# A hybrid attention layer on one core: other signs in its seven-product matrix form, one weight sum made by an adding transfer, and three reorderings in attention

## The chip, the core and the metric

The kernel runs on one core of a Trainium2 chip. The core has a matrix engine (PE, with its weight loads shown apart as PEld), a vector engine (DVE), a scalar engine (ACT), a general engine (POOL) and SyncE (SP), each with its own instruction queue; they meet at semaphores. Weights come from device memory by DMA into SBUF, matmuls write PSUM, and DVE and ACT read both. The metric is the device time of one execution in microseconds (us): 362.66 us before the change, the median of three runs from 362.60 to 362.94.

## The reference

One decoder layer in float32: RMSNorm, one wide projection, two attention mixers (NSA: compressed, selected and sliding-window keys; MoBA: block sparse), gates, an output projection, and a feed-forward block with squared ReLU between two more norms. There are 256 tokens and a model width of 1024.

```python
h = rmsnorm(x, norm1_g[layer])
proj = h @ w_in[layer]
...
gm = jax.nn.sigmoid(g_m.astype(jnp.float32)).astype(x.dtype)
g_nsa = gm[..., :D_MODEL]
g_moba = gm[..., D_MODEL:]
mixed = g_nsa * (y_nsa @ w_up_nsa[layer]) + g_moba * (y_moba @ w_up_moba[layer])
x = x + mixed @ w_out[layer]
h2 = rmsnorm(x, norm2_g[layer])
u = jax.nn.relu(h2 @ w_ff1[layer])
x = x + (u * u) @ w_ff2[layer]
...
return rmsnorm(x, norm_f_g)
```

With 256 tokens all selected and windowed keys lie within the causal mask, so the kernel computes two causal softmaxes per NSA head and one per MoBA head.

## The kernel before, in words

**Exact float32 from three products.** Each weight chunk (`raw`, 1 MB, three buffers, loaded by SP) is split in two: ACT copies a rounded part into `whi` (line 114), DVE subtracts it and leaves the rest in `wlo` (line 116). The activations are split the same way, and PE does three matmuls per block: hi by hi, hi by lo, lo by hi.

**Slots.** The program is a list of slots, one per weight chunk (`CHUNKS`): `kva`, `kvb`, `q`, `qm`, `km`, `vm`, eight `gm`, `upn`, `upm`, four `wout`, then the feed-forward chunks. `run_slot` issues a slot's matmuls one after another; everything else (splits, copies, loads, attention) is put among them by `at(pos, f, ...)`: it is issued when the share `pos` of the slot's matmuls has been issued, and ties keep the order of writing. No scheduler changes this: every engine runs its instructions in that order, and an instruction that waits holds up what stands behind it on its engine.

**Early part.** After the `kva` chunks, `evac_tm` copies each half of the accumulator twice over into `kcd` (line 326) and the rest into `kva` (line 329). `cmp_gather` (line 419) turns `kcd` on PE, `gather_evac` adds position terms on DVE.

**Attention.** Six units `d` of two heads' pairs each run through slots 9 to 21 (`unit_events`, line 648): in an odd slot scores on PE (`d_scores`), maxima on DVE, exponentials on ACT (line 581), and the product with the values of the unit before (`d_pv`, `d_yevac`); in the even slot after it the normalising on DVE (`d_norm`, line 595) and the transposes on PE (`d_trans`, line 611), whose results ACT (line 613) and DVE (line 615) copy back. Slot 9 holds the second `km` chunk, slot 12 the first `gm` chunk. At half of slot 9, `evac_tm` copies the first half of MoBA's keys from PSUM (line 329, `qtm`) and frees an accumulator that the `vm` chunk needs.

**Feed-forward.** An ff1 slot (48 matmuls of 256 columns) makes 256 hidden columns; ACT squares them (`squares`, tile `aq`). The product with `w_ff2` is done for the first 14 chunks by a form of two-by-two block multiplication with seven products in place of eight (`SEVEN`, line 1011): sums of blocks of `aq` and sums of weight blocks (`sums`, line 974) are multiplied, the seven products pile up in seven PSUM banks over all 14 chunks, and `combine` (line 1028) adds them into the output once at the end. So each pair of slots (a seven-product slot and an ff1 slot) has on DVE: the weight sums into tile `wt` (lines 984, 988, 990), the activation sums (line 982), the rest `sl` of the single blocks (line 999), the rest of the ff1 chunk (line 116), the rest of `wt` (line 1008) and the rest `al` of the activations (line 958). ACT makes the rounded parts (lines 997, 114, 1006, 956). `wt` has two buffers, as have `sh`, `sl`, `ah`, `al`; `whi` and `wlo` have three. The last two ff2 chunks are multiplied in the plain way, and the output is normalised (`final_a`, `final_b`; the power is done on POOL, line 1171) and stored.

```python
    SEVEN = (("1", 0, 0), ("7", 4, 4), ("5", 3, 3), ("6", 5, 5), ("2", 2, 1), ("3", 6, 2),
             ("4", 1, 6))
```

Each entry is a product's name, the index of the block of `A` (blocks 1 to 7 of `aq`, split) and of the weight block (0 to 2 the single blocks, 3 to 6 those of `wt`).

Of the kernel before, what the change touches and what calls it, by code (L numbers as in the profile page):

```python
# [8 lines left out]
F32 = mybir.dt.float32  # L9
F32R = mybir.dt.float32r  # L10
AF = mybir.ActivationFunctionType
ALU = mybir.AluOpType
# [9 lines left out]
NSEVEN = 14  # L22
# [23 lines left out]
def hybrid_layer(ctx: ExitStack, tc: tile.TileContext, gxd, w, w1c, small, const, gf, out):  # L46
# [178 lines left out]
    def at(pos, f, *a):  # L225
        ev.append((pos, f, a))
# [94 lines left out]
    vm = ap_.tile([128, 2, 512], F32, name="vm")  # L321
    tm = {"kva": kva, "kvb": kvb, "vm": vm}

    def evac_tm(sec, t, acc, n):
        if sec == "kva":
            act.activation(kcd[:, t], acc[:, 0:256].rearrange("p (a d) -> p a d", a=4)[:, :, None, :]
                           .to_broadcast([128, 4, 2, 64]), AF.Copy, scale=rstd[:, t:t + 1])
            acc, n = acc[:, 256:384], 128
        act.activation(tm[sec][:, t, :], acc[:, :n], AF.Copy, scale=rstd[:, t:t + 1])  # L329

# [317 lines left out]
    def unit_events(s):  # L648
        d = (s - 9) // 2
        if not 9 <= s <= 21:  # L650
            return
        if s % 2 == 0:
            at(0.1, d_norm, d)
            at(0.97 if s == 12 else 0.78, d_trans, d)
            return
        if d < 6:
            at(0.1, d_scores, d)
        if d > 0:
            at(0.1, d_pv, d - 1)
        if d < 6:  # L660
            at(0.11, d_max, d)
            at(0.2 if s > 12 else 0.5, d_exp, d, 1)
            at(0.22 if s > 12 else 0.52, d_exp, d, 0)
        if d > 0:
            at(0.12, d_yevac, d - 1)


    groups = [("kva", 0, 384), ("kvb", C_KVB, 408), ("q", C_Q, 512), ("qm", C_QM, 512),
# [1 line left out]
    for sec, c0, n in groups:  # L670
# [6 lines left out]
        for i in range(2):  # L677
            c = c0 + i
            if c == 0:
                at(0.6, load, 5)  # L680
            elif c == 1:
                at(0.88, row_squares, 0)
                for k in range(4):
                    at(0.89, split, 2, k, 4)
                for k in range(1, 4):
                    at(1.1, row_squares, k)
                at(1.1, row_sums, 0, 2, 2)
                at(1.1, row_sums, 4, 6, 2)
                at(1.1, row_sums, 0, 4, 2)
                at(1.1, row_sums, 0, 1, 1)  # L690
                for k in range(4):
                    at(1.2, split, 3, k, 4, "h")
                for k in range(2):
                    at(1.3, split, 3, k, 4, "l")

            elif c == 2:
                at(0.9, row_norm)
                for k in range(2, 4):
                    at(0.91, split, 3, k, 4, "l")
                at(0.92, load, 6)  # L700
                at(0.92, nc.sync.dma_start, w1, w1c)
            elif c == 3:
                for k in range(2):
                    at(0.0, split, 4, k, 2, "h")
                for t in range(2):
                    at(0.01, evac_tm, "kva", t, first[t], 384)
                for k in range(2):
                    at(0.1, split, 4, k, 2, "l")
                at(0.11, load, 7)
                at(0.66, cmp_gather)  # L710
                for k in range(2):
                    at(0.66, gather_evac, k)
                for k in range(2):
                    at(0.7, split, 5, k, 2, "h")
            elif c == 4:
                for t in range(2):
                    at(0.0, evac_tm, "kvb", t, second[t], 408)
                at(0.1, split, 5, 0, 2, "l")
                at(0.2, rope, kva, 2)
                at(0.3, split, 5, 1, 2, "l")  # L720
                at(0.35, load, 8)
                split_events(c, (0.5, 0.55), (0.8, 0.9))
                at(0.7, cmp_mlp1)
            else:
                std_events(c)
# [33 lines left out]
            if c == 1:  # L759
                first = accs  # L760
            elif c == 3:
                second = accs
            elif i == 1:
                at(0.49 if sec == "vm" else 0.5, evac_tm, sec, 0, accs[0], n)
                if sec != "vm":
                    at(1.0, evac_tm, sec, 1, accs[1], n)
            run_slot(xstat(c, n, accs, range(4 * i, 4 * i + 4)))
# [206 lines left out]
    def sums(c):  # L974

        b = raw[c].rearrange("p (b n) -> p b n", b=4)
        T = FB["p"].tile([128, 4, 512], F32, name="wt", bufs=2)
        W[c] = T
        aq = A[CHUNKS[c][1]][0]

        def a_sum(o, x, y, op):
            dve.tensor_tensor(aq[:, o], aq[:, x], aq[:, y], op=op)  # L982

        dve.tensor_tensor(T[:, 0:2], b[:, 1:4:2], b[:, 0, None, :].to_broadcast([128, 2, 512]),  # L984
                          op=ALU.subtract)
        a_sum(4, 0, 2, ALU.add)
        a_sum(5, 1, 0, ALU.subtract)
        dve.tensor_tensor(T[:, 2], b[:, 3], T[:, 0], op=ALU.add)  # L988
        a_sum(6, 4, 1, ALU.subtract)
        dve.tensor_tensor(T[:, 3], b[:, 2], T[:, 2], op=ALU.subtract)  # L990
        a_sum(7, 3, 6, ALU.subtract)

    def w_singles(c, which):
        v = raw[c][:, 512:2048]
# [6 lines left out]
    def w_parts(c, which):  # L1001
# [5 lines left out]
        else:  # L1007
            dve.tensor_tensor(lo[c], v, hi[c].bitcast(F32), op=ALU.subtract)  # L1008


    SEVEN = (("1", 0, 0), ("7", 4, 4), ("5", 3, 3), ("6", 5, 5), ("2", 2, 1), ("3", 6, 2),
             ("4", 1, 6))
    P = {}

# [13 lines left out]
    def combine(step):  # L1028

        fst, x1, scr = FB["fst"], FB["x1"], FB["scr"]  # L1030
        u, v = scr[:, 0:512], scr[:, 512:1024]
        lo_, hi_ = slice(0, 512), slice(512, 1024)

        def into(t, s, y):
            dve.scalar_tensor_tensor(x1[:, t, s], y, fst[:, 4 + t:5 + t], x1[:, t, s],
                                     op0=ALU.mult, op1=ALU.add)

        if step == 0:
            act.activation(u, P["6"], AF.Copy)
            into(1, lo_, P["1"])  # L1040
            dve.tensor_tensor(u, P["1"], u, op=ALU.add)
        elif step == 1:
            dve.tensor_tensor(v, u, P["5"], op=ALU.subtract)
            dve.tensor_tensor(u, u, P["7"], op=ALU.add)
            into(0, lo_, u)
        else:
            into(1, hi_, v)
            dve.tensor_tensor(v, v, P["7"], op=ALU.add)
            into(0, hi_, v)

    PARTS = {0: [(0, 0, 512), (0, 512, 512)], 1: [(1, 0, 512), (1, 512, 512)]}
# [17 lines left out]
    def slot_events(c):  # L1069

        if seven(c + 2):
            if c + 2 == C_FF + 3:
                at(0.1, w_singles, c + 2, "h")
                at(0.12, sums, c + 2)
                at(0.15, w_parts, c + 2, "h")
                at(0.2, w_singles, c + 2, "l")
                at(0.3, load, c + 5)
                at(0.35, w_parts, c + 2, "l")
            else:
                at(0.01, w_parts, c + 2, "h")  # L1080
                at(0.1, w_parts, c + 2, "l")
                at(0.4, act_parts, CHUNKS[c + 2][1], "h")
                at(0.6, act_parts, CHUNKS[c + 2][1], "l")
        elif c + 2 < NCH - 1:
# [23 lines left out]
            at(0.76, act_parts, 14, "l")  # L1108

    fst, x1, scr = None, None, None  # L1110
    for c in range(C_FF, NCH - 2):
        sec, i, _ = CHUNKS[c]
        if c == C_FF:
# [176 lines left out]
```

## Time and profile before

| | before |
|---|---|
| median of three runs | 362.66 us (362.60 to 362.94) |
| the profiled execution | 362.55 us |
| its span (first to last instruction) | 360.7 us |
| granted PE clock, mean | 0.996 |
| DMA traffic | 66.34 MB, mean 184 GB/s |
| POOL busy | 3.4 us, 14 instructions |

Each row of a timeline gives the start, the duration, the engine, the line of the kernel, the operation, the tile written and the tiles read, and in brackets how long the engine stood idle before it and what released it. Durations of neighbours on one engine overlap a little, so the step from one start to the next is the better measure of what an instruction costs.

### The profile page before, as it was taken

What the parts mean: (1) busy time and instruction counts of PE and PEld (TensorE: products, weight loads), DVE (VectorE), ACT (ScalarE), POOL (GpSimd) and SP (SyncE); (2) the same over time, 40 slices, a digit from 0 to 9 for tenths busy, and PEclk for the clock granted to TensorE, in tenths of its full rate; (3) what the DMA queues carried; (4) which work ended last, traced back from release to release, by engine and by line L of the source; (5) the groups of instructions that cost most, each with busy time, mean ns of one, the idle gap of its engine ahead of it and who ended that gap; (6) DMA issues with size and microseconds to landing.
All of it is one profiled execution on the core that took longest, in us unless ns stands there. A gap on an engine that the chain in (4) does not pass through costs nothing.

```text
span 360.7 us, 6539 instructions
## 1 busy us (share of the span) xinstructions
PE 350.6 (97%) x2663; PEld 326.2 (90%) x2663; DVE 320.0 (89%) x470; ACT 244.0 (68%) x367; POOL 3.4 (1%) x14
## 2 busy tenths in 40 slices
PE   8999999999999999999999999999999999999992
PEld 7997888888999999999999999999999999999972
DVE  4898889998966859767969999999999999999984
ACT  5995865777755757436366979768666678677623
POOL 1010000000000000000000000000000000000000
PEclk9999999999999999999999999999999999999998
DMA  8988425334533335433595466544455666544003
GB/s 276 405 330 314 165 79 224 116 118 144 203 122 118 118 118 171 180 118 116 204 323 197 155 233 234 212 175 187 171 201 223 233 234 231 183 180 186 38 3 116
DMA packets 11262, 66.34 MB, mean 184 GB/s; under 512 B 1248, under 2 KB 2784, under 8 KB 3936
## 3 DMA queue, kind: packets, MB, share of 16 engines
q1 hardware_dynamic: 10368, 64.35, 48.4%
q10 hardware_dynamic: 864, 1.57, 1.2%
q8 instruction: 21, 0.34, 0.4%
q14 instruction: 9, 0.07, 0.1%
HBM read 64.87 MB, written 1.05 MB: 183 GB/s over the span
## 4 chain that ended last, share of the span: by engine, by line
PE 50%; DVE 39%; issue 4%; ACT 3%; DMA 1%; SPq 0%; POOLq 0%; DVEq 0%; POOL 0%; ACTq 0%
PE acc L255 35%; DVE wlo L116 10%; DVE wlo L1008 6%; DVE sl L999 5%; DVE al L958 3%; DVE wt L984 3%; PE qacc L255 3%; PE yb L255 3%; DVE aq L982 3%; PE kvbacc L255 2%; ACT P L581 2%; DVE wt L988 2%; PE o L255 1%; DMA gx<-in_gx_dram 1%; PE Sa L611 1%
## 5 line engine op out<-in xcount | busy, mean ns | idle before, releaser
L114 ACT ACTIVATE whi<-raw 128x1024 fp32r<-128x1024 f32 (+3 forms) x82 | 90.0, 1119 | 33.3 <-DMA raw<-in_ff_dram 17.6
L116 DVE TENSOR_TENSOR wlo<-raw,whi 128x1024 fp32r<-128x1024 f32 (+3 forms) x83 | 105.2, 1290 | 2.8 <-ACT whi L114 2.6
L255 PE MATMUL acc<-h2h,wlo 128*128 128x256 f32 x256 | 71.4, 279 | 0.4
L255 PE MATMUL acc<-h2h,whi 128*128 128x256 f32 x256 | 70.5, 275 | 0.0
L255 PE MATMUL acc<-h2l,whi 128*128 128x256 f32 x256 | 70.4, 275 | 0.0
L255 PEld LDWEIGHTS acc<-h2h,wlo 128*128 128x128 f32 x256 | 49.1, 192 | 2.2 <-DVE wlo L116 2.1
L255 PEld LDWEIGHTS acc<-h2l,whi 128*128 128x128 f32 x256 | 49.2, 192 | 0.0
L255 PEld LDWEIGHTS acc<-h2h,whi 128*128 128x128 f32 x256 | 49.1, 192 | 0.0
L1006 ACT ACTIVATE whi<-wt 128x2048 fp32r<-128x2048 f32 x14 | 26.9, 1920 | 19.6 <-DVE wt L990 17.7
L255 PE MATMUL acc<-hTh,wlo 128*128 128x256 f32 x128 | 36.2, 283 | 0.0
L255 PE MATMUL acc<-hTl,whi 128*128 128x256 f32 x128 | 35.3, 276 | 0.0
L255 PE MATMUL acc<-hTh,whi 128*128 128x256 f32 x128 | 35.2, 275 | 0.0
L1008 DVE TENSOR_TENSOR wlo<-wt,whi 128x2048 fp32r<-128x2048 f32 x14 | 32.3, 2306 | 0.1
L255 PE MATMUL acc<-whi,hTh 128*128 128x512 f32 (+2 forms) x65 | 24.7, 380 | 0.5 <-ACT qtm L329 0.5
L999 DVE TENSOR_TENSOR sl<-raw,sh 128x1536 fp32r<-128x1536 f32 x14 | 24.8, 1771 | 0.0
L255 PEld LDWEIGHTS acc<-hTh,wlo 128*128 128x128 f32 x128 | 24.6, 192 | 0.2 <-issue 0.2
L255 PEld LDWEIGHTS acc<-hTh,whi 128*128 128x128 f32 x128 | 24.6, 192 | 0.1
L255 PEld LDWEIGHTS acc<-hTl,whi 128*128 128x128 f32 x128 | 24.6, 192 | 0.0
L255 PE MATMUL acc<-wlo,hTh 128*128 128x512 f32 (+2 forms) x65 | 24.5, 376 | 0.1
L255 PE MATMUL acc<-whi,hTl 128*128 128x512 f32 (+2 forms) x65 | 24.1, 371 | 0.0
L997 ACT ACTIVATE sh<-raw 128x1536 fp32r<-128x1536 f32 x14 | 20.7, 1479 | 0.0
L255 PE MATMUL acc<-mxl,whi 128*128 128x256 f32 x64 | 17.7, 276 | 0.0
(310 smaller groups left out, 872.0 us busy)
## 6 DMA issues: line engine op xcount, KB each, us to landing
raw<-in_ff_dram SPq DMA_DIRECT2D x32, 1024.0 KB, 5.2
raw<-in_gm_dram SPq DMA_DIRECT2D x8, 1024.0 KB, 4.8
raw<-in_wout_dram SPq DMA_DIRECT2D x4, 1024.0 KB, 4.8
raw<-in_q_dram SPq DMA_DIRECT2D x2, 1024.0 KB, 5.2
raw<-in_qm_dram SPq DMA_DIRECT2D x2, 1024.0 KB, 6.4
raw<-in_km_dram SPq DMA_DIRECT2D x2, 1024.0 KB, 6.1
raw<-in_vm_dram SPq DMA_DIRECT2D x2, 1024.0 KB, 4.7
raw<-in_upn_dram SPq DMA_DIRECT2D x2, 1024.0 KB, 4.9
```

The costliest lines, as they stand in the source:

```text
L114: act.activation(hi[c][:, a:b], raw[c][:, a:b], AF.Copy)
L116: dve.tensor_tensor(lo[c][:, a:b], raw[c][:, a:b], hi[c][:, a:b].bitcast(F32), op=ALU.subtract)
L255: pe.matmul(o, l, r, start=start, stop=stop, skip_group_check=True)
L581: act.activation(P[:, 2 * x + j, a:b], S[:, j, x], AF.Exp, scale=0.125, bias=st[:, 1, i:i + 1], accum_out=st[:, 2, i:i + 1])
L958: dve.tensor_tensor(A[i][2][:, 0:b - a], aq[:, a:b], A[i][1][:, 0:b - a].bitcast(F32), op=ALU.subtract)
L982: dve.tensor_tensor(aq[:, o], aq[:, x], aq[:, y], op=op)
L984: dve.tensor_tensor(T[:, 0:2], b[:, 1:4:2], b[:, 0, None, :].to_broadcast([128, 2, 512]), op=ALU.subtract)
L988: dve.tensor_tensor(T[:, 2], b[:, 3], T[:, 0], op=ALU.add)
L997: act.activation(singles[c][0], v, AF.Copy)
L999: dve.tensor_tensor(singles[c][1], v, singles[c][0].bitcast(F32), op=ALU.subtract)
L1006: act.activation(hi[c], v, AF.Copy)
L1008: dve.tensor_tensor(lo[c], v, hi[c].bitcast(F32), op=ALU.subtract)
```

## The change

**Seven-product form.** The four weight sums were `b1 - b0`, `b3 - b0`, `b3 + (b1 - b0)` and `b2 - (b3 + b1 - b0)`. They are now `b1 + b0`, `b3 + b0`, `b3 + (b1 + b0)` and `b2 + (b3 + b1 + b0)`, with signs in the activation sums and in `combine` to match, and the two first sums in exchanged order in `SEVEN`. The sum `b3 + b0` (`wt[:, 1]`) is no longer made by DVE: `sum_load` has POOL transfer block 3 from device memory into it and then block 0 with an adding transfer. The other three stay on DVE. The activation sums are three instructions instead of four, the first of them with 256 columns. `sum_load` is called for chunks 0 and 1 ahead of the feed-forward part and then two chunks ahead, after the last reader of the buffer. Since `wt` is now allocated first, `ur`, `aq`, `sh` and `sl` lie 16 KB higher in SBUF and `wt` lower.

**Early copies.** The two `kcd` copies of slot 3 come before the second `whi` split of that slot, and the gather's transposes two matmuls later.

**MoBA keys.** The copy of the first half of `km` is issued at 0.49 of its slot instead of 0.5, which puts it before the exponentials that stand at 0.5.

**Second pair.** The transposes of unit 1 move from 0.97 of slot 12 to 0.01 of slot 13, and slot 13's scores, maxima, exponentials and value product move back by 0.22.

```diff
+    def evac_twice(t, acc):
+        act.activation(kcd[:, t], acc[:, 0:256].rearrange("p (a d) -> p a d", a=4)[:, :, None, :]
+                       .to_broadcast([128, 4, 2, 64]), AF.Copy, scale=rstd[:, t:t + 1])
+
     def evac_tm(sec, t, acc, n):
         if sec == "kva":
-            act.activation(kcd[:, t], acc[:, 0:256].rearrange("p (a d) -> p a d", a=4)[:, :, None, :]
-                           .to_broadcast([128, 4, 2, 64]), AF.Copy, scale=rstd[:, t:t + 1])
             acc, n = acc[:, 256:384], 128
...
         if s % 2 == 0:
             at(0.1, d_norm, d)
-            at(0.97 if s == 12 else 0.78, d_trans, d)
+            if s != 12:
+                at(0.78, d_trans, d)
             return
+        late = 0.22 if s == 13 else 0
+        if s == 13:
+            at(0.01, d_trans, d - 1)
         if d < 6:
-            at(0.1, d_scores, d)
+            at(0.1 + late, d_scores, d)
         if d > 0:
-            at(0.1, d_pv, d - 1)
+            at(0.1 + late, d_pv, d - 1)
...
             elif c == 3:
-                for k in range(2):
-                    at(0.0, split, 4, k, 2, "h")
+                at(0.0, split, 4, 0, 2, "h")
+                for t in range(2):
+                    at(0.0, evac_twice, t, first[t])
+                at(0.0, split, 4, 1, 2, "h")
...
-                at(0.66, cmp_gather)
+                at(0.72, cmp_gather)
...
-                at(0.49 if sec == "vm" else 0.5, evac_tm, sec, 0, accs[0], n)
+                at(0.49 if sec in ("km", "vm") else 0.5, evac_tm, sec, 0, accs[0], n)
...
-        T = FB["p"].tile([128, 4, 512], F32, name="wt", bufs=2)
-        W[c] = T
+        T = W[c]
         aq = A[CHUNKS[c][1]][0]
-
-        def a_sum(o, x, y, op):
-            dve.tensor_tensor(aq[:, o], aq[:, x], aq[:, y], op=op)
-
-        dve.tensor_tensor(T[:, 0:2], b[:, 1:4:2], b[:, 0, None, :].to_broadcast([128, 2, 512]),
+        dve.tensor_tensor(T[:, 0], b[:, 1], b[:, 0], op=ALU.add)
+        dve.tensor_tensor(aq[:, 4:6], aq[:, 1:3], aq[:, 0, None, :].to_broadcast([128, 2, 128]),
                           op=ALU.subtract)
-        a_sum(4, 0, 2, ALU.add)
-        a_sum(5, 1, 0, ALU.subtract)
         dve.tensor_tensor(T[:, 2], b[:, 3], T[:, 0], op=ALU.add)
-        a_sum(6, 4, 1, ALU.subtract)
-        dve.tensor_tensor(T[:, 3], b[:, 2], T[:, 2], op=ALU.subtract)
-        a_sum(7, 3, 6, ALU.subtract)
+        dve.tensor_tensor(aq[:, 6], aq[:, 1], aq[:, 5], op=ALU.add)
+        dve.tensor_tensor(T[:, 3], b[:, 2], T[:, 2], op=ALU.add)
+        dve.tensor_tensor(aq[:, 7], aq[:, 3], aq[:, 6], op=ALU.subtract)
+
+    def sum_load(i):
+
+        if i < NSEVEN:
+            T = W[C_FF + 3 + 2 * i] = FB["p"].tile([128, 4, 512], F32, name="wt", bufs=2)
+            pool.dma_start(T[:, 1], w["ff2"][i, :, 1536:2048])
+            pool.dma_start(T[:, 1], w["ff2"][i, :, 0:512], accum_op=ALU.add)
...
-    SEVEN = (("1", 0, 0), ("7", 4, 4), ("5", 3, 3), ("6", 5, 5), ("2", 2, 1), ("3", 6, 2),
+    SEVEN = (("1", 0, 0), ("7", 3, 4), ("5", 4, 3), ("6", 5, 5), ("2", 2, 1), ("3", 6, 2),
              ("4", 1, 6))
...
-            dve.tensor_tensor(u, P["1"], u, op=ALU.add)
+            dve.tensor_tensor(u, P["1"], u, op=ALU.subtract)
         elif step == 1:
-            dve.tensor_tensor(v, u, P["5"], op=ALU.subtract)
+            dve.scalar_tensor_tensor(v, u, -1.0, P["5"], op0=ALU.mult, op1=ALU.subtract)
...
-            dve.tensor_tensor(v, v, P["7"], op=ALU.add)
+            dve.tensor_tensor(v, v, P["7"], op=ALU.subtract)
...
                 at(0.35, w_parts, c + 2, "l")
+                at(0.36, sum_load, 2)
             else:
                 at(0.01, w_parts, c + 2, "h")
                 at(0.1, w_parts, c + 2, "l")
+                at(0.11, sum_load, CHUNKS[c + 2][1] + 2)
...
+    for i in range(2):
+        sum_load(i)
     for c in range(C_FF, NCH - 2):
```

What this moves on the engines is seen from the order of their instructions (line, operation, tile written and tiles read, size; "x4" is four in a row). The changed kernel's lines are numbered a few higher: 999, 1006, 1008, 958 become 1008, 1015, 1017, 966.

One pair of slots on DVE, in the middle of the feed-forward part, before:

```order
L999 TENSOR_TENSOR sl<-raw,sh 128x1536
L116 TENSOR_TENSOR wlo<-raw,whi 128x2048
L1008 TENSOR_TENSOR wlo<-wt,whi 128x2048
L958 TENSOR_TENSOR al<-aq,ah 128x896
L984 TENSOR_TENSOR wt<-raw 128x1024
L982 TENSOR_TENSOR aq<-aq 128x128 x2
L988 TENSOR_TENSOR wt<-raw,wt 128x512
L982 TENSOR_TENSOR aq<-aq 128x128
L990 TENSOR_TENSOR wt<-raw,wt 128x512
L982 TENSOR_TENSOR aq<-aq 128x128
```

and the same pair now:

```order
L1008 TENSOR_TENSOR sl<-raw,sh 128x1536
L116 TENSOR_TENSOR wlo<-raw,whi 128x2048
L1017 TENSOR_TENSOR wlo<-wt,whi 128x2048
L966 TENSOR_TENSOR al<-aq,ah 128x896
L987 TENSOR_TENSOR wt<-raw 128x512
L988 TENSOR_TENSOR aq<-aq 128x256
L990 TENSOR_TENSOR wt<-raw,wt 128x512
L991 TENSOR_TENSOR aq<-aq 128x128
L992 TENSOR_TENSOR wt<-raw,wt 128x512
L993 TENSOR_TENSOR aq<-aq 128x128
```

The order stays; the first weight sum has half its columns, and two activation sums have become one of twice the size.

POOL's queue between the rows for the first norm and the final one was empty. It now holds 14 pairs of transfers, of which the first six rows are these, with the semaphores that each waits for (DMASW are those of POOL's own transfers):

```order
L999 DMA wt<-in_ff_dram 128x512 [waits DVE_49,PE_49,DMAHW2_49,Activation_49,Pool_49]
L1000 DMA wt<-in_ff_dram 128x512 [waits DMASW0_49]
L999 DMA wt<-in_ff_dram 128x512
L1000 DMA wt<-in_ff_dram 128x512 [waits DMASW2_49]
L999 DMA wt<-in_ff_dram 128x512 [waits DMASW1_49,DVE_49]
L1000 DMA wt<-in_ff_dram 128x512 [waits DMASW4_49]
```

Each adding transfer (line 1000) waits for the plain one before it to land; from the third pair on, the plain one waits for DVE to have read the buffer, by the row of line 1017 of two chunks before.

In slot 9 on ACT (`qmh` are MoBA's queries, `P` the exponentials of unit 0, `qtm` here MoBA's keys), before:

```order
L373 ACTIVATE qmh<-tp 128x512 x2
L581 ACTIVATE P,ust<-Sa,ust 128x256 x4
L329 ACTIVATE qtm<-acc,rstd 128x512
L581 ACTIVATE P,ust<-Sb,ust 128x128 x4
L329 ACTIVATE qtm<-acc,rstd 128x512
```

and now:

```order
L375 ACTIVATE qmh<-tp 128x512 x2
L331 ACTIVATE qtm<-acc,rstd 128x512
L583 ACTIVATE P,ust<-Sa,ust 128x256 x4
L583 ACTIVATE P,ust<-Sb,ust 128x128 x4
L331 ACTIVATE qtm<-acc,rstd 128x512
```

The first copy of the keys has moved ahead of the four long exponentials. On PE, around the end of slot 12, unit 1's twelve transposes (`Sa`, `Sb` from `P`) stand two matmuls later, and 15 matmuls instead of 6 lie between them and the next unit's scores.

More of the change, by code (lines that the diff above doesn't have):

```diff
@@ L653, in unit_events @@
             at(0.1, d_norm, d)
-            at(0.97 if s == 12 else 0.78, d_trans, d)
+            if s != 12:
+                at(0.78, d_trans, d)
             return
+        late = 0.22 if s == 13 else 0
+        if s == 13:
+            at(0.01, d_trans, d - 1)
         if d < 6:
-            at(0.1, d_scores, d)
+            at(0.1 + late, d_scores, d)
         if d > 0:
-            at(0.1, d_pv, d - 1)
+            at(0.1 + late, d_pv, d - 1)
         if d < 6:
-            at(0.11, d_max, d)
-            at(0.2 if s > 12 else 0.5, d_exp, d, 1)
-            at(0.22 if s > 12 else 0.52, d_exp, d, 0)
+            at(0.11 + late, d_max, d)
+            at(0.2 + late if s > 12 else 0.5, d_exp, d, 1)
+            at(0.22 + late if s > 12 else 0.52, d_exp, d, 0)
         if d > 0:
-            at(0.12, d_yevac, d - 1)
+            at(0.12 + late, d_yevac, d - 1)
     groups = [("kva", 0, 384), ("kvb", C_KVB, 408), ("q", C_Q, 512), ("qm", C_QM, 512),
@@ L709, in hybrid_layer @@
                 at(0.11, load, 7)
-                at(0.66, cmp_gather)
+                at(0.72, cmp_gather)
                 for k in range(2):
-                    at(0.66, gather_evac, k)
+                    at(0.72, gather_evac, k)
                 for k in range(2):
```

## The prediction

> **What bounds the kernel now.** I read the page's summary and the chain that ended last first, then busy time by stretch, then the rows of single engines where the chain changes hands.
>
> ```profile
> span 360.7 us, 6539 instructions
> PE 350.6 (97%) x2663; PEld 326.2 (90%) x2663; DVE 320.0 (89%) x470; ACT 244.0 (68%) x367; POOL 3.4 (1%) x14
> PE 50%; DVE 39%; issue 4%; ACT 3%; DMA 1%; SPq 0%; POOLq 0%; DVEq 0%; POOL 0%; ACTq 0%
> ```
>
> PE looks full (97%), yet only half of the chain runs through it and 39% through DVE. Matmuls overlap, so a busy PE can still be paced by another engine. Where that happens is seen by cutting the feed-forward part into its pairs (a seven-product slot and an ff1 slot), each from the first matmul `o<-sh,ah` to the next. The windows' columns are busy time and count of PE, PEld, DVE, ACT, POOL, then the granted clock, the DMA share and GB/s:
>
> ```profile
> 245.96:256.19 10.23, 10.19 (x75) 9.51 (x74) 10.23 (x13) 7.40 (x6) 0.00 (x0) 1.00 0.55 207
> 206.15:216.06 9.91, 9.91 (x73) 9.40 (x72) 9.91 (x12) 7.85 (x7) 0.00 (x0) 1.00 0.55 212
> PEld acc L255 <- DVE wlo L116: 2.8, 12, 0.4
> 235.89 0.38 PE L255 MATMUL o<-sh,ah 128*128 128x512 f32 x1
> 337.96 0.38 PE L255 MATMUL o<-sh,ah 128*128 128x512 f32 x1
> ```
>
> An early pair takes 9.91 us, a later one 10.23, at the same clock (1.00). In the later ones DVE is busy for the whole pair and PE's weight loads wait for `wlo` of line 116, which DVE makes. From 235.89 to 337.96 lie ten pairs: 102.07 us, or 2.97 more than 10 x 9.91 (the first, up to 245.96, takes 10.07, the nine after it 10.22 each). So **PE alone needs 9.91 us a pair and DVE 10.22**.
>
> **Part 1, the seven-product form: a DVE pair gets shorter.** One DVE pair of before, up to the next pair's `sl` (columns: start, duration, engine, line; the time between two starts is what an instruction costs, since the shown durations overlap a little):
>
> ```profile
> 238.38 2.29 DVE L116 TENSOR_TENSOR wlo<-raw,whi 128x2048 fp32r<-128x2048 f32 x1
> 240.58 2.29 DVE L1008 TENSOR_TENSOR wlo<-wt,whi 128x2048 fp32r<-128x2048 f32 x1
> 242.78 1.10 DVE L958 TENSOR_TENSOR al<-aq,ah 128x896 fp32r<-128x896 f32 x1
> 243.78 1.23 DVE L984 TENSOR_TENSOR wt<-raw 128x1024 f32<-128x1024 f32 x1
> 244.92 0.50 DVE L982 TENSOR_TENSOR aq<-aq 128x128 f32<-128x128 f32 x2
> 245.32 0.70 DVE L988 TENSOR_TENSOR wt<-raw,wt 128x512 f32<-128x512 f32 x1
> 245.92 0.30 DVE L982 TENSOR_TENSOR aq<-aq 128x128 f32<-128x128 f32 x1
> 246.12 0.70 DVE L990 TENSOR_TENSOR wt<-raw,wt 128x512 f32<-128x512 f32 x1
> 246.72 0.30 DVE L982 TENSOR_TENSOR aq<-aq 128x128 f32<-128x128 f32 x1
> 246.93 1.77 DVE L999 TENSOR_TENSOR sl<-raw,sh 128x1536 fp32r<-128x1536 f32 x1
> ```
>
> The two-block sum of line 984 costs 1.14 us (243.78 to 244.92); as one block it is the size of line 988, 0.60. That saves **0.54**. Four sums of 128 columns (0.40 + 0.20 + 0.20) become one of 256 and two of 128. A 256-column one is not in this stage; another (below) shows 0.42 us, of which some 0.09 overlaps with the next as in line 988's row (0.70 shown, 0.60 from start to start). That makes 0.33, so 0.73 in place of 0.80, a gain of **0.07**.
>
> ```profile
> 77.64 0.42 DVE L646 TENSOR_TENSOR yTln<-yb,yThn 128x256 fp32r<-128x256 f32 x1
> ```
>
> DVE then needs 10.22 - 0.61 = 9.61 us a pair, below PE's 9.91, and PE becomes the bound: **-2.95 us** by the ten pairs above, and no more than that, whatever else DVE saves. The combine's three sign edits keep engine, 512 columns and operands' places (one takes another form of instruction) and run once; I put them at 0, an estimate from the equal size, 0.1 at most either way.
>
> What replaces the sum is two transfers of 256 KB per pair, the second waiting on POOL for the first and adding to it. No transfer from POOL and no adding transfer is in the trace of before. Bounds for one of them are the shortest and longest landings there:
>
> ```profile
> out_dram<-gx SPq DMA_DIRECT2D x3, 192.0 KB, 1.9
> w<-in_w_dram SPq DMA_DIRECT2D x1, 1024.0 KB, 6.8
> gx<-in_gx_dram SPq DMA_DIRECT2D x3, 256.0 KB, 5.0
> raw<-in_ff_dram SPq DMA_DIRECT2D x32, 1024.0 KB, 5.2
> ```
>
> So two in a row take 3.8 to 13.6 us; I take 10, from the 256 KB row. Their cover: the buffer `wt` is one of two and free when line 1008 has read it (242.78); the block is next read by ACT's `whi<-wt`, two pairs later. That loop is transfers + 1.92 (ACT row below) + 2.20 (line 1008) + some 0.2 of hand-over, against two pairs of 9.91, so the transfers are hidden up to 15.5 us. Queued behind the waiting POOL is only the next transfer, and long after them the final norm's power. The first two wait for the last reader of the attention's memory, line 832, whose last row ends at 171.18, and are needed by line 1006 at 197.47: 26 us of cover. The transfers add 0.5 MB to a pair's 2 MB; at the windows' share of 0.55 that makes about 0.7 of the DMA time. A `raw` load may land some 0.7 us later (1024 KB in 5.2 us is 1.3 us for 256 KB, half of it shared). ACT would feel it, DVE not: the ff1 split ends at 235.0 on ACT and DVE uses it at 238.38.
>
> ```profile
> 170.35 0.83 DVE L832 SCALAR_TENSOR_TENSOR mxl<-sga,mxh 128x256 fp32r<-128x256 f32 x2 [0.86 <-ACT mxh L827]
> 197.47 1.93 ACT L1006 ACTIVATE whi<-wt 128x2048 fp32r<-128x2048 f32 x1 [0.99 <-DVE wt L990]
> 233.08 1.93 ACT L114 ACTIVATE whi<-raw 128x2048 fp32r<-128x2048 f32 x1 [1.07 <-DMA raw<-in_ff_dram]
> 236.69 1.91 ACT L1006 ACTIVATE whi<-wt 128x2048 fp32r<-128x2048 f32 x1 [1.68 <-DVE wt L990]
> ```
>
> **Part 2, what a DVE that is ahead gives at the end.** With 0.3 us a pair DVE runs ahead of PE until a buffer stops it. ACT's line 1006 needs a `whi` that PE frees at the end of an ff1 slot (235.89), so it can move up 0.8 us at most and end at 237.8; DVE's line 1008 uses it at 240.58. The lead can grow to about 2.8 us. The tail uses it:
>
> ```profile
> 339.58 0.58 ACT L1039 ACTIVATE fscr<-o 128x512 f32<-128x512 f32 x1
> 341.42 0.72 DVE L1041 TENSOR_TENSOR fscr<-o,fscr 128x512 f32<-128x512 f32 x1
> 342.54 0.63 ACT L956 ACTIVATE ah<-aq 128x512 fp32r<-128x512 f32 x1 [2.38 <-PE tp L255]
> 344.43 0.69 DVE L958 TENSOR_TENSOR al<-aq,ah 128x512 fp32r<-128x512 f32 x1
> 344.01 0.38 PE L255 MATMUL tp<-wlz,ah 128*128 128x512 f32 x1
> 345.17 0.48 PE L255 MATMUL tp<-whz,al 128*128 128x512 f32 x1 [0.78 <-DVE al L958]
> ```
>
> The copy that line 1041 reads ends at 340.16, but DVE comes to it at 341.42, 1.26 late; line 958 could start at 343.2 and starts at 344.43. PE loses 345.17 - 344.23 = 0.94 there. From 1041 on DVE is dense almost to the end, so both engines move up: 0.94 on PE, up to 1.2 on DVE. I take **-1.1**; bounds 0 (no lead at the end) and -1.2.
>
> **Part 3, attention.** Copying MoBA's keys before the first exponentials removes a wait; the second pair's transposes move behind two more matmuls:
>
> ```profile
> 63.02 0.38 PE L255 MATMUL acc<-whi,hTl 128*128 128x512 f32 x1
> 63.88 0.48 PE L255 MATMUL acc<-whi,hTh 128*128 128x512 f32 x1 [0.49 <-ACT qtm L329]
> 81.92 1.29 DVE L407 TENSOR_TENSOR hTl<-hn,hTh 128x512 fp32r<-128x512 f32 x2 [1.00 <-ACT hTh L405]
> 85.12 0.28 PE L255 MATMUL acc<-hTl,whi 128*128 128x256 f32 x1
> 85.73 1.09 PE L611 MATMUL Sa<-ident,P 128*128 128x128 f32 x8 [0.33 <-DVE P L595]
> ```
>
> PE's step at 63.02 takes 0.86 where its neighbours take 0.22: 0.64 lost. That gain doesn't last whole, since the first pair's transposes then wait for DVE's `P`; I carry 0.42 past them. The value copies, exponentials and `hTh` behind it move up as much, DVE's wait of 1.00 before `hTl` shrinks, and line 595 ends 0.42 earlier. The second transposes still wait, but two matmuls of 0.11 now lie ahead of them (0.22), and the scores behind 15 matmuls instead of 6 no longer wait for the evictions (about 0.1). Sum **-0.75**; bounds -0.3 (DVE's `P` doesn't move) and -1.0 (all of both waits). The early compression copies and the later gather are put at 0: between 23 and 63 us PE shows no wait there to remove, and DVE's delay of some 0.4 us is taken up by slack behind it.
>
> **The sum** against the profiled execution, 362.55 us (its span 360.7 and 1.85 around it; 0.11 below the median of 362.66): -2.95 - 1.1 - 0.75 = -4.8, so 357.75, beside the median 357.86. I say **357.8**.
>
> **Rivals.**
> *A: the lead does not build up.* Some hand-over keeps DVE level with PE; only 2.95 + 0.75 come: 358.9. For it: ACT already waits 1.07 us for a `raw`. Against: the slacks of 2.8 and 3.4 us above.
> *B: the adding transfers are late.* Above 15.5 us for two they set the pace. At 18 us a pair takes (18 + 4.3) / 2 = 11.15; the 13 pairs of 206 to 338 took 131.8 and would take 145: about 375. Against it: that needs 9 us each, above every landing listed.
> *C: slower, because POOL's transfer work holds up DVE.* Both use SBUF; if each transfer costs DVE x, its pair is 9.61 + 2x, and beyond x = 0.36 the 13 pairs lose more than attention gains and 0.7 besides. At x = 0.97, POOL's longest row, a pair takes 11.55, 13 of them 150.2: about 380. Against it: that POOL row lies beside four splits of DVE (two of 408 columns, two of 1024), and they show no stretch (3.34 us; two pairs alone take 1.07 and 2.35).
>
> ```profile
> 18.87 0.97 POOL L220 TENSOR_TENSOR rstd<-stat,mhalf 128x2 f32<-128x2 f32 x1 [16.89 <-DVE stat L219]
> 18.70 3.34 DVE L116 TENSOR_TENSOR wlo<-raw,whi 128x408 fp32r<-128x408 f32 x4
> ```
>
> It is weak evidence, since that row moves next to no data. The Trainium skill, "SBUF — State Buffer", section "Who interferes with whom", says that DVE and GpSimd share one port pair under an exclusive lock, but that a DVE instruction with two SBUF inputs clashes only with a GpSimd instruction that reads SBUF, and infers that making descriptors only writes. By that rule C costs nothing here, as the row suggests; by the lock alone it would be C's 380. No run here shows a POOL transfer yet.
> *D: nothing comes of it.* DVE loses 0.3 us per transfer, and its pair is again 10.2: 361.9 with attention.
>
> **Chances.** Forecast 0.64 (357.0 to 358.5), A and a partial lead 0.19 (358.5 to 360.5), B 0.04, C 0.08, D 0.05. Faster by over 0.2% (below 361.9, about what a measurement here can tell from no change) 0.83, within it 0.05 (D), slower 0.12 (B and C). The range for 8 in 10 is 356.9 to 360.5.
>
> **What would show it.** Pairs of 9.91 us and no wait of PEld on line 116 in the feed-forward part; DVE at some 97% there, now waiting for others; no PE wait on `al` near the end; no PE wait on `qtm`; POOL's transfers landing long before `whi<-wt`. Wrong, if DVE's rows grow while POOL issues, if ACT's `whi<-wt` waits for a DMA, or if pairs stay above 9.95.

## The result and the profile after

The changed kernel takes **358.94 us** (median of 20 runs, 358.23 to 363.09) against 362.64 before (20 runs, 362.22 to 363.98): a ratio of 0.9899, 95% interval 0.9882 to 0.9915. Predicted were 357.8, with a range of 356.9 to 360.5. The profiled execution took 359.07 us. Its summary, and the engines' shares of the chain that ended last:

```profile
span 357.3 us, 6572 instructions
PE 347.7 (97%) x2663; PEld 324.7 (91%) x2663; DVE 312.0 (87%) x456; ACT 242.0 (68%) x367; POOL 23.7 (7%) x42
PE 72%; DVE 10%; DMA 8%; issue 5%; ACT 3%; POOL 0%; SPq 0%; POOLq 0%; DVEq 0%; ACTq 0%
```

PE now carries 72% of the chain (50% before), DVE 10% (39%), and DMA 8% (1%). Two rows of PE's timeline bound the ten pairs that the prediction rested on; with them one pair in the view by stretches (columns as there), and one DVE pair from `sl` to the next `sl`:

```profile
235.54 0.38 PE L255 MATMUL o<-sh,ah 128*128 128x512 f32 x1
334.82 0.38 PE L255 MATMUL o<-sh,ah 128*128 128x512 f32 x1
245.46:255.37 9.91, 9.91 (x74) 9.43 (x73) 9.38 (x11) 7.21 (x6) 1.44 (x2) 1.00 0.83 256
```

```profile
255.10 1.75 DVE L1008 TENSOR_TENSOR sl<-raw,sh 128x1536 fp32r<-128x1536 f32 x1
256.76 2.28 DVE L116 TENSOR_TENSOR wlo<-raw,whi 128x2048 fp32r<-128x2048 f32 x1
258.97 2.29 DVE L1017 TENSOR_TENSOR wlo<-wt,whi 128x2048 fp32r<-128x2048 f32 x1
261.17 1.08 DVE L966 TENSOR_TENSOR al<-aq,ah 128x896 fp32r<-128x896 f32 x1
262.17 0.69 DVE L987 TENSOR_TENSOR wt<-raw 128x512 f32<-128x512 f32 x1
262.77 0.42 DVE L988 TENSOR_TENSOR aq<-aq 128x256 f32<-128x256 f32 x1
263.11 0.69 DVE L990 TENSOR_TENSOR wt<-raw,wt 128x512 f32<-128x512 f32 x1
...
264.72 1.75 DVE L1008 TENSOR_TENSOR sl<-raw,sh 128x1536 fp32r<-128x1536 f32 x1
```

The ten pairs take 99.28 us (102.07 before), nine of them 9.91 to 9.92 and one 10.04. A dense DVE pair takes 264.72 - 255.10 = 9.62. In the stretch DVE is busy 9.38 of 9.91, and the DMA engines 0.83 where they were 0.55.

The tail, in rows of ACT, DVE and PE: ACT's copy of product "6", the sum that reads it, `ah` and `al` of the last block, and the matmul that waited for `al`:

```profile
336.44 0.58 ACT L1048 ACTIVATE fscr<-o 128x512 f32<-128x512 f32 x1
337.57 0.68 DVE L1050 TENSOR_TENSOR fscr<-o,fscr 128x512 f32<-128x512 f32 x1
340.55 0.69 DVE L966 TENSOR_TENSOR al<-aq,ah 128x512 fp32r<-128x512 f32 x1
340.87 0.38 PE L255 MATMUL tp<-wlz,ah 128*128 128x512 f32 x1
341.29 0.48 PE L255 MATMUL tp<-whz,al 128*128 128x512 f32 x1
```

DVE comes to line 1050 0.55 us after its operand (1.26 before), and PE's step before `al` is 0.42 in place of 1.16, of which 0.22 is a matmul. The combine's edited signs cost nothing: the one instruction that took another form (line 1052) steps on after 0.79 us, as its forerunner did before.

**The transfers are the surprise.** First the sums of waits (us in total, times, longest), then the issues by line with the median from issue to landing, then one buffer's round (POOL's two issues, ACT's copy, DVE's subtraction, and the next issue into the same buffer):

```profile
POOL wt L1000 <- DMA wt<-in_ff_dram: 78.8, 14, 8.6
ACT whi L1015 <- DMA wt<-in_ff_dram: 25.9, 10, 3.2
raw<-in_ff_dram SPq DMA_DIRECT2D x32, 1024.0 KB, 6.5
wt<-in_ff_dram POOLq DMA_DIRECT2D x28, 256.0 KB, 6.6
291.79 0.56 POOL L999 DMA_DIRECT2D wt<-in_ff_dram  x1 [3.05 <-DVE wlo L1017]
298.17 0.87 POOL L1000 DMA_DIRECT2D wt<-in_ff_dram  x1 [5.81 <-DMA wt<-in_ff_dram]
306.97 1.92 ACT L1015 ACTIVATE whi<-wt 128x2048 fp32r<-128x2048 f32 x1 [3.22 <-DMA wt<-in_ff_dram]
308.92 2.29 DVE L1017 TENSOR_TENSOR wlo<-wt,whi 128x2048 fp32r<-128x2048 f32 x1 [0.39 <-ACT whi L1015]
311.51 0.56 POOL L999 DMA_DIRECT2D wt<-in_ff_dram  x1 [2.54 <-DVE wlo L1017]
```

The plain transfer takes 298.17 - 291.79 = 6.4 us, the adding one 306.97 - 298.17 = 8.8: **15.2 for two**, where the prediction took 10 and named 15.5 as the limit. The round shown is 311.51 - 291.79 = 19.72 us, against two pairs of 9.91. It is one of several: in the ten rounds in which ACT's copy waits for the landing, the two transfers take 14.5 to 15.9 us, and the ten rounds that begin between 202 and 292 us take 19.44 to 20.42, 19.83 on average, which is just two pairs. So the transfers stand at the limit, on both sides of it. The one pair of 10.04 us is that in which ACT's copy starts latest, after two transfers of 15.87.

**Where the time went, stage by stage.** Four marks cut a trace: ACT's copy of `qT` near 40 us (start and first projections lie ahead), the matmul `o<-sh,ah` of the second pair, that of the last pair, and DVE's last scaling. The first and last of the changed kernel:

```profile
40.74 0.59 ACT L366 ACTIVATE qT<-tp 128x512 f32<-128x512 f32 x1
352.51 0.75 DVE L1192 TENSOR_SCALAR gx<-gx,fst 128x384 f32<-128x384 f32 x2 [0.66 <-POOL fst L1184]
```

| kernel (profiled execution) | start to `qT` | `qT` to second pair | 13 pairs | last pair to last scaling | scaling to end of span |
|---|---|---|---|---|---|
| before | 40.24 | 165.91 | 131.81 | 18.56 | 4.18 |
| changed | 40.74 | 165.07 | 129.01 | 17.69 | 4.79 |
| changed, again | 39.97 | 165.13 | 129.47 | 17.58 | 4.75 |
| three buffers | 40.07 | 165.12 | 128.89 | 17.49 | 4.63 |
| without the adding | 39.97 | 165.00 | 128.89 | 17.50 | 4.24 |
| sum on DVE | 40.54 | 165.11 | 130.85 | 18.55 | 4.15 |
| sum on DVE, transfers idle | 40.23 | 165.14 | 132.34 | 18.44 | 4.75 |
| attention undone | 40.91 | 165.90 | 128.89 | 17.27 | 4.73 |
| transposes undone | 40.38 | 165.51 | 128.89 | 17.26 | 4.76 |

The last column goes by spans that are known to 0.1 us. Attention gained 0.84, the pairs 2.80, the tail 0.87: 4.51 us. The start of this execution came 0.50 late, which varies from trace to trace (the other kernels with the changed start lie on both sides of 40.24), and the end takes 0.6 more: the span is 3.4 shorter.

### The profile page after: what moved, and what is told of

The parts are those of the page before. It is cut to its first block, busy times and chain, and to the rows that moved or that the text cites. A ratio compares the mean times of both kernels' runs of the same rounds, so it can differ in the third digit from the quotient of the medians.

```text
span 357.3 us, 6572 instructions
## 1 busy us (share of the span) xinstructions
PE 347.7 (97%) x2663; PEld 324.7 (91%) x2663; DVE 312.0 (87%) x456; ACT 242.0 (68%) x367; POOL 23.7 (7%) x42
## 4 chain that ended last, share of the span: by engine, by line
PE 72%; DVE 10%; DMA 8%; issue 5%; ACT 3%; POOL 0%; SPq 0%; POOLq 0%; DVEq 0%; ACTq 0%
PE acc L255 47%; PE o L255 7%; DMA wt<-in_ff_dram 6%; PE yb L255 5%; PE qacc L255 3%; PE kvbacc L255 3%; PE tp L255 2%; DVE wlo L116 2%; PE Sa L613 2%; DMA gx<-in_gx_dram 2%; PE Sa L255 1%; DVE wlo L1017 1%; ACT whi L1015 1%; PE tp L355 1%; PE Sb L613 1%
## 5 line engine op out<-in xcount | busy, mean ns | idle before, releaser
L255 PE MATMUL acc<-h2h,wlo 128*128 128x256 f32 x256 | 70.4, 275 | 0.0
L1015 ACT ACTIVATE whi<-wt 128x2048 fp32r<-128x2048 f32 x14 | 26.9, 1918 | 27.6 <-DMA wt<-in_ff_dram 25.9
L999 POOL DMA_DIRECT2D wt<-in_ff_dram x14 | 8.4, 598 | 199.0 <-PE acc L255 151.3
```

The costliest lines, as they stand in the source:

```text
L255: pe.matmul(o, l, r, start=start, stop=stop, skip_group_check=True)
L999: pool.dma_start(T[:, 1], w["ff2"][i, :, 1536:2048])
L1015: act.activation(hi[c], v, AF.Copy)
```

## The experiments

My theory after this reading: the terms of the prediction are right, the transfers are slower than taken and hold back the lead of DVE. Rivals: another buffer holds it; the transfers cost DVE something; attention's gain is lost again later.

**Attention undone.** All edits ahead of the feed-forward part go back to the lines of before:

```diff
-                at(0.49 if sec in ("km", "vm") else 0.5, evac_tm, sec, 0, accs[0], n)
+                at(0.49 if sec == "vm" else 0.5, evac_tm, sec, 0, accs[0], n)
...
-            if s != 12:
-                at(0.78, d_trans, d)
+            at(0.97 if s == 12 else 0.78, d_trans, d)
```

> The changed kernel with all its attention edits taken back (MoBA keys' copy, second pair's transposes, early compression copies and later gather as in the kernel before); the feed-forward part stays changed. My theory: the attention edits are worth 0.75 us, nearly all of it from the keys' copy, so this kernel takes about 359.7 us (changed kernel 358.94), PE's matmul at about 63 us waits again for the eviction (0.6 us lost there), and the feed-forward part is as in the changed kernel. Rival: what attention gains is lost again before the feed-forward part or in its buffers; then 358.9, no difference.

Measured 359.68 us (359.29 to 360.65; 0.992 of before, 0.9901 to 0.9938), 0.74 above the changed kernel. `qT` to second pair is 165.90, as before, and PE's wait is back. First the two rows of the changed kernel, where the step is 0.21, then those of this run, where it is 0.86:

```profile
63.41 0.38 PE L255 MATMUL acc<-whi,hTl 128*128 128x512 f32 x1
63.62 0.38 PE L255 MATMUL acc<-whi,hTh 128*128 128x512 f32 x1
```

```profile
63.69 0.38 PE L255 MATMUL acc<-whi,hTl 128*128 128x512 f32 x1
64.55 0.48 PE L255 MATMUL acc<-whi,hTh 128*128 128x512 f32 x1 [0.48 <-ACT qtm L329]
```

The rival that attention gains nothing in the end falls.

**Transposes undone**, the keys' copy kept:

```diff
-            if s != 12:
-                at(0.78, d_trans, d)
+            at(0.97 if s == 12 else 0.78, d_trans, d)
...
-            at(0.1 + late, d_scores, d)
+            at(0.1, d_scores, d)
```

> The changed kernel with the second pair's transposes and the work behind them back at their old places; the keys' copy and the early copies stay changed. My theory: of attention's 0.75 us this is 0.3 (0.22 and 0.1), so from ACT's copy of qT at 40 us to the first matmul o<-sh,ah of the second pair the trace shows 165.4 us (165.07 in the changed kernel, 165.9 without any attention edit), and the time is about 359.2. Rival: the keys' copy alone brings all of it: 165.1 and 358.9.

Measured 359.24 us (358.29 to 360.21), and 165.51 in the trace: the transposes and what stands behind them bring 0.44, and the keys' copy, with the early copies that this run keeps too, 165.90 - 165.51 = 0.39. The runs' spread is wider than this difference; it is the trace that separates them, and the eleven traces with all of the changed attention lie between 164.87 and 165.15 there.

**The sum back on DVE, no transfers:**

```diff
-        dve.tensor_tensor(T[:, 0], b[:, 1], b[:, 0], op=ALU.add)
+        dve.tensor_tensor(T[:, 0:2], b[:, 1:4:2], b[:, 0, None, :].to_broadcast([128, 2, 512]),
+                          op=ALU.add)
...
-            pool.dma_start(T[:, 1], w["ff2"][i, :, 1536:2048])
-            pool.dma_start(T[:, 1], w["ff2"][i, :, 0:512], accum_op=ALU.add)
```

> The changed kernel with the moved sum back on DVE (one instruction for two blocks) and no transfers; signs, sums of 256 columns and attention edits stay. My theory: DVE's pair is 9.62 + 0.54 = 10.16 us against PE's 9.91, ten pairs lose 2.5 us and the tail its stall of about 0.75, so about 362.2 us; 1 MB loads in the feed-forward part land in 5.2 us again instead of 6.5. Rival: the transfers cost something themselves (memory traffic, POOL's part), so that leaving them out gives back part of what DVE's sum costs: below 361.

**The same with the transfers running idle**, into a fifth block of `wt`:

```diff
+            pool.dma_start(T[:, 4], w["ff2"][i, :, 1536:2048])
+            pool.dma_start(T[:, 4], w["ff2"][i, :, 0:512], accum_op=ALU.add)
```

> As with the sum on DVE (361.15 us), but both transfers run as in the changed kernel, into a fifth block of the same buffer that nothing reads: the output is whole, and the transfers' own cost stands alone. My theory: they cost DVE nothing (its pair stays 10.15 to 10.16 us), only the 1 MB loads land some 1.3 us later, and the end of the program gets the 0.55 us longer that all kernels with 28 of these transfers show (4.6 to 4.8 us from DVE's last scaling to the end of the span, against 4.15 to 4.24 with none or 14): 361.7 us. Rival 1 (POOL's transfer work or the traffic slows DVE): a pair of 10.2 us or more and 362.3 or more. Rival 2 (the long end was chance): 361.15.

Without transfers 361.15 us (360.48 to 361.47), with idle ones 362.61 (361.72 to 363.96). One late pair in the stretches of each, first without, then with transfers:

```profile
265.42:275.58 10.16, 10.16 (x75) 9.51 (x73) 10.16 (x11) 7.47 (x6) 0.00 (x0) 1.00 0.56 206
```

```profile
266.62:276.78 10.16, 10.16 (x75) 9.51 (x73) 10.16 (x11) 7.40 (x6) 1.43 (x2) 1.00 0.82 243
206.28 0.48 PE L255 MATMUL o<-sh,al 128*128 128x512 f32 x1 [0.32 <-DVE al L966]
```

DVE is busy for the whole pair in both, and the pair is 10.16 us as worked out, though POOL issues (1.43 us) and the DMA share is 0.82 against 0.56. So **the transfers take nothing from DVE**; in the range of 240 to 330 us DVE's 2048-column splits average 2.309 us in the kernel before, 2.283 without transfers and 2.302 with them, and the 0.02 between the last two does not show in the pair. The trace agrees with what the Trainium skill, "SBUF — State Buffer", "Who interferes with whom", marks as inferred: that a DVE instruction reading two operands from SBUF does not clash with making descriptors. Yet the idle transfers cost 1.46 us by the medians of two chips (1.7 by the two spans), not 0.55: the end is 0.6 longer, and the first and third of its 13 pairs take 10.49 and 10.39 us (the second 9.91). The row at 206.28 shows the first stall: PE waits for a late `al`, and DVE, with its lead spent, paces PE from the third pair on; without transfers the first four pairs take 9.90 to 9.92. The time is in the range of rival 1, but its pair is not. Expectation and rivals both missed this: a cost at one place, where the feed-forward part begins.

The forecast without transfers was 1 us too high: the run's end is 0.6 shorter than the changed kernel's, and DVE holds PE up from the fifth pair on only, so the 13 pairs lose 1.84 and not 2.5.

**Without the adding transfer** (so one sum is missing from one of the seven products), and **three buffers**, with nothing left out:

```diff
-            pool.dma_start(T[:, 1], w["ff2"][i, :, 0:512], accum_op=ALU.add)
```

> The changed kernel without the adding transfer: block 1 of the sums holds one weight block alone, so one sum is missing from one of the seven products. My theory: transfers (6.4 + 8.8 us) plus ACT's 1.95, DVE's 2.3 and 0.3 between them make a loop of 19.7 us, just under two pairs of 9.91, and this is what keeps DVE from running ahead. Without the second the loop is 11 us: ACT's 25.9 us of waits for the transfer fall below 5, DVE comes to the first sum of the combine when its operand is ready (0.55 us late in the changed kernel), PE's last 0.2 us before the final products goes, and the time falls by 0.3 to 0.6, to about 358.5. Rival: another buffer holds DVE level with PE; then the waits move to it and the time stays at 358.9.

```diff
-            T = W[C_FF + 3 + 2 * i] = FB["p"].tile([128, 4, 512], F32, name="wt", bufs=2)
+            T = W[C_FF + 3 + 2 * i] = FB["p"].tile([128, 4, 512], F32, name="wt", bufs=3)
...
-                at(0.11, sum_load, CHUNKS[c + 2][1] + 2)
+                at(0.11, sum_load, CHUNKS[c + 2][1] + 3)
```

> The changed kernel with three buffers instead of two for the sums, so that the transfers for a pair start one pair earlier; nothing is left out. My theory: as without the adding transfer, since the loop of 19.7 us now has three pairs (29.7): ACT no longer waits for the transfers, the tail gains 0.3 to 0.6, about 358.5 us. Rival 1 (another buffer sets the lead): 358.9. Rival 2 (the traffic itself slows the 1 MB loads, which hold ACT up instead): ACT's waits move to the weight loads and the time stays within 0.1 of 358.9, while without the adding transfer it falls.

Measured 357.91 us without the adding (357.40 to 358.08) and 358.18 with three buffers (357.97 to 359.18). In both ACT's wait for the transfers is gone from the sums of waits, and PE's matmuls, which free `whi`, are in its place, first without the adding, then with three buffers:

```profile
ACT whi L1014 <- PE acc L255: 26.7, 12, 2.6
```

```profile
ACT whi L1015 <- PE acc L255: 22.0, 12, 2.6
335.69 0.58 ACT L1048 ACTIVATE fscr<-o 128x512 f32<-128x512 f32 x1
336.42 0.68 DVE L1050 TENSOR_TENSOR fscr<-o,fscr 128x512 f32<-128x512 f32 x1
```

DVE now comes to the sum of the combine 0.15 us after its operand, the tail is 17.49 to 17.50 and all 13 pairs together take 128.89. This is the stop that the prediction expected (a `whi` that PE frees), and it is reached when the transfers no longer stop DVE before it. The 1 MB loads still land in 6.6 us with three buffers, so the traffic is not what held DVE. The time without the adding is below the forecast of 358.5 because the end is shorter too (4.24 against 4.63 with three buffers).

Two buffers can reach the same, though. With the transposes undone (two buffers, 28 transfers) ACT still waits 20.5 us for the transfers, and yet the 13 pairs take 128.89 and DVE comes to the sum 0.14 us after its operand:

```profile
ACT whi L1011 <- DMA wt<-in_ff_dram: 20.5, 8, 3.3
336.39 0.58 ACT L1044 ACTIVATE fscr<-o 128x512 f32<-128x512 f32 x1
337.11 0.68 DVE L1046 TENSOR_TENSOR fscr<-o,fscr 128x512 f32<-128x512 f32 x1
339.36 0.63 ACT L960 ACTIVATE ah<-aq 128x512 fp32r<-128x512 f32 x1 [2.38 <-PE tp L255]
```

So the sum of ACT's waits does not tell what lead DVE has at the end. ACT's last copy of the sums starts 0.31 us after the mark of its pair there, with three buffers 0.09 and in the changed kernel 1.12. The tail is even shorter there, 17.26 against 17.49. DVE's lead is the same, but ACT's `ah` starts 4.58 us after the last pair's mark, with three buffers and in the changed kernel 4.86, each time released by PE's `tp`. Why PE releases it 0.28 us later in some kernels stays open.

**Both once more on one chip:**

> The changed kernel as it stands, once more, beside the three-buffer one on the same chip: 358.9 us.

> Three buffers for the sums once more, beside the changed kernel on the same chip. My theory (the lead was held by the transfers): 0.3 to 0.8 us below the changed kernel, some 358.2 us. Rival (the 358.18 of the first run was a good start by chance): equal to the changed kernel.

358.9 us (358.72 to 359.25) and 358.59 (357.93 to 360.56): ratios to before of 0.9899 (0.9885 to 0.9914) and 0.9895 (0.9874 to 0.9917). By time, three buffers are 0.3 to 0.8 better by the medians of two comparisons, and the intervals overlap; the traces show the gain, the times do not settle it. The changed kernel's second trace holds the early stall too:

```profile
206.01 0.48 PE L255 MATMUL o<-sh,al 128*128 128x512 f32 x1 [0.32 <-DVE al L966]
```

Its first of 13 pairs takes 10.49. Ahead of it the first transfers meet the 1 MB loads of the first feed-forward blocks. The stretch from 180 to 190 us, before and changed:

```profile
180.00:190.00 10.00, 10.00 (x92) 10.00 (x91) 7.00 (x15) 7.18 (x11) 0.00 (x0) 1.00 0.85 306
```

```profile
180.00:190.00 10.00, 10.00 (x92) 10.00 (x92) 6.08 (x12) 5.95 (x10) 0.88 (x1) 1.00 1.00 359
185.71 1.06 ACT L114 ACTIVATE whi<-raw 128x1024 fp32r<-128x1024 f32 x1 [3.17 <-DMA raw<-in_ff_dram]
```

The DMA engines are full (1.00), and ACT waits 3.17 us for a load where it waited 1.14 before. What is late there is made up in some executions (the profiled one: first pair 9.90; three buffers: 9.91, after a wait of 3.04 for the same load) and not in others. That the first transfers cause the stall is argued and not shown: no kernel without them has it, and of those with 28 some have it and some don't. It fits that the changed kernel's times spread more upward; moving the first transfers was not tried.

**A third transfer**, adding one more weight block (of the seven products only "7" reads block 1 of the sums and is off by it, and `combine` adds it into two blocks of the output):

```diff
             pool.dma_start(T[:, 1], w["ff2"][i, :, 0:512], accum_op=ALU.add)
+            pool.dma_start(T[:, 1], w["ff2"][i, :, 512:1024], accum_op=ALU.add)
```

> The changed kernel with a second adding transfer behind the first, so that block 1 of the sums holds one weight block too many (two of the seven products are off by it). My theory: the loop of a buffer becomes 6.4 + 8.8 + 8.8 + 4.5 = 28.5 us for two pairs, so a pair takes 14.2 us instead of 9.91 once the two buffers loaded ahead are used up: 12 pairs lose 4.3 us each, about 411 us, with PE waiting in every pair. If transfers land faster when the loads come more seldom (a third of 5 us): (6.4 + 5 + 5 + 4.5) / 2 = 10.45, about 365.5. Rival: transfers overlap with each other and the cover of 15.5 us is no limit: 359 to 360.

Measured 411.2 us (409.52 and 412.89). Two pairs take 27.74 us (28.5 forecast), and PE stands still behind ACT, ACT behind the transfers:

```profile
286.60:314.34 27.74, 21.98 (x146) 20.83 (x145) 19.08 (x21) 14.47 (x12) 4.60 (x6) 0.88 0.72 208
ACT whi L1016 <- DMA wt<-in_ff_dram: 82.1, 12, 11.6
PE acc L255 <- ACT ur L953: 40.6, 7, 8.3
```

So the limit is real, and the changed kernel, whose rounds are 19.83 us on average, stands at it.

**The second transfer plain**, overwriting the first (block 1 holds one weight block alone):

```diff
-            pool.dma_start(T[:, 1], w["ff2"][i, :, 0:512], accum_op=ALU.add)
+            pool.dma_start(T[:, 1], w["ff2"][i, :, 0:512])
```

> The changed kernel with the second transfer plain instead of adding, so that it overwrites the first: block 1 of the sums holds one weight block alone. Same bytes from memory, same serial order. My theory: adding is what makes the second transfer slow (8.5 us from issue to landing against 6.1 for the first, and about twice the DMA time per byte), so without it both land in 4 to 5.5 us, the loop is 14 us or less, ACT no longer waits for the transfers (25.9 us in the changed kernel) and the time is that without the adding transfer, 357.9 to 358.3. Rival: the second is slow because of what else runs then (the 1 MB loads); then it stays at 8 us and the time at 358.9.

The second lands in 6.3 us (median; the adding one 8.5), the first in 5.0 (6.1), and ACT's wait for them is gone (20.3 us of waits for PE instead). So adding costs some 2 us here. The rest, above the 4.0 us that the one plain transfer per pair took without the adding one, would then come from the traffic around it; no run separates that further. The time, 358.8 us (358.25 to 359.64), was not the 357.9 to 358.3 expected: its trace has the early stall at its largest, a first pair of 10.90, and is that of its longest execution (359.64). The queue's lines (packets, MB, share of 16 engines), changed kernel and this one:

```profile
q0 software_dynamic: 3136, 7.34, 9.6%
```

```profile
q0 software_dynamic: 2240, 7.34, 7.9%
```

**Other queues for the plain transfer**, with three buffers: SP's, or ACT's from the fourth pair on.

```diff
-            pool.dma_start(T[:, 1], w["ff2"][i, :, 1536:2048])
+            nc.sync.dma_start(T[:, 1], w["ff2"][i, :, 1536:2048])
```

> Three buffers for the sums as before (358.18 us), and the plain transfer of each pair issued on SP's queue behind the 1 MB loads instead of on POOL; POOL keeps the 14 adding ones. My theory: what lengthens the end by some 0.5 us is POOL's program with 28 transfers, so with 14 the end is 4.2 us again and the time about 357.7; the plain transfer lands later behind the 1 MB loads, which three buffers hide. Rival 1: the end depends on the transfers' traffic or on adding, not on their number on POOL: 358.2. Rival 2: the plain transfer holds up the 1 MB loads on its queue, ACT waits more for them and the time is over 358.5.

```diff
-            pool.dma_start(T[:, 1], w["ff2"][i, :, 1536:2048])
+            (act if i > 2 else pool).dma_start(T[:, 1], w["ff2"][i, :, 1536:2048])
...
-                at(0.11, sum_load, CHUNKS[c + 2][1] + 3)
+                at(0.9, sum_load, CHUNKS[c + 2][1] + 3)
```

> Three buffers, and from the fourth pair on the plain transfer is issued by ACT at the end of a pair, when the buffer has long been read; POOL has 17 transfers in place of 28. My theory: the end is 0.45 us shorter as with 14 or none, ACT's 11 issues of some 0.4 us fit its idle time, about 357.7 us. Rival 1: the end stays long (17 are enough for it): 358.2. Rival 2: ACT's issues push its copies back and DVE waits for them: 358.5 or more.

359.55 us (357.50 to 366.58) and 358.65 (358.18 to 359.11): neither is better. On SP's queue the 1 MB loads land in 7.7 us, and the times scatter. The trace with ACT's queue has the early stall once more (first pair 10.48). The end of the span was the aim: 4.36 and 4.58 us after the last scaling, with 14 and 17 transfers on POOL. With the third transfer, 42 of them on POOL, it is 4.34. So the number of transfers does not set the long end.

## Why the prediction came out as it did

- **Part 1, DVE's pair**: predicted 9.61 us, measured 9.62. PE became the bound at 9.91, as forecast, and with the sum back on DVE the pair is 10.16; the ten pairs gained 2.79 of 2.95, and all of it with three buffers (128.89 for 13 pairs, 9.91 each).
- **Part 1, the transfers: the term that was mis-sized.** Two were put at 10 us from the 5.0 of a plain 256 KB load at the start of the program; they take 15.2 in the round shown and 14.5 to 15.9 in all the rounds where ACT waits for them, since they run beside 1 MB loads (those slowed from 5.2 to 6.5, where about 0.7 was estimated) and because adding itself costs some 2 us. The bounds (3.8 to 13.6) did not hold the value, and a sign that the prediction named for being wrong came true: `whi<-wt` waited for a DMA, 25.9 us in ten waits. The limit of 15.5 did its work: the third transfer shows what lies beyond it. That two transfers came out at the limit and not past it is luck, since nothing in the working put them there and not at 17 us.
- **"ACT would feel it, DVE not"** was wrong at the beginning of the part, where loads and first transfers fill the DMA engines and `al` came late (0.58 us in the second trace of the changed kernel, 0 in the first).
- **Part 2**: -0.87 measured, -1.1 predicted. The lead was 0.4 us short (0.55 against 0.15 after the operand) where ACT's last copies waited for the adding transfer; with three buffers the gain is 18.56 - 17.49 = 1.07. With attention or the transposes undone the two buffers were enough, and the gain is 1.29 and 1.30, past the bound of 1.2, so the round sits at the edge and falls on either side. Single traces don't tell whether the kernel or the execution decides that.
- **Part 3**: -0.75 predicted, -0.84 in the trace, -0.74 by time; 0.42 for the keys' copy was 0.39, 0.32 for the rest 0.44: the wait of the second transposes, which the prediction kept, is gone from the trace of the changed kernel.
- **Not in the sum**: some 0.55 us at the very end of the span, and the early stall. The profiled execution (359.07) is 1.3 us above 357.75: the late start 0.50, the end 0.6, the tail 0.23 and the pairs 0.15 too long, attention 0.09 better. The second trace (358.72) is 1.0 above: the pairs, with the stall, 0.6, the end 0.6, the tail 0.1, less 0.3 for an early start.
- **Rivals**: A came in part, by the transfers, and 358.94 lies in its part of the chances (358.5 to 360.5, 0.19), not in the forecast's. B's law holds (third transfer: 27.74 us for two pairs), and its condition, two transfers above 15.5, was met in some rounds and not in others. C and D are refuted by the pair of 10.16 us with and without transfers. C's bound of 0.36 is not what its own terms give: 13 pairs of 9.61 + 2x lose 0.75 + 0.7 from x = 0.32 on.

## What to carry to other kernels

Work taken off a saturated engine is worth what that engine is behind, and no more; the step is settled by two rows, the pair of each engine. A transfer that replaces an instruction has a round (issue, landing, reader, release), and that round, in the traffic that will then run and not in that of a quiet stretch, is to be held against the buffers' turn: here the round was as long as the turn, 19.8 us. A third buffer took ACT's waits for the transfers away in both of its traces; the times don't yet show what that is worth. Whether the first transfers should keep clear of the stretch where other loads fill the DMA engines is the next thing to try.

## What the hardware showed that was not expected

- An adding transfer of 256 KB from POOL's queue took 8.5 us (median) from issue to landing beside 1 MB loads, a plain one in its place 6.3, and a plain one that was alone in its pair 4.0.
- The kernels with 28 transfers from POOL end 4.6 to 4.8 us after DVE's last scaling, those with none or 14 end 4.15 to 4.4 after, though the last output transfers land in 2.2 to 2.4 us in both kinds; with 17 it is 4.58, with 42 it is 4.34. What makes it stays open.
